# Rotary embedding of 16 heads: two of the early loads are issued in two halves each

## The chip, the core and the metric

The kernel runs on one core of a Trainium2 chip. Its time is device microseconds (us) of one launch; the time before is the median of three runs, 161.38 us (161.21 to 161.65). The core has five engines that matter here: TensorE (PE in the profile; PEld are its weight loads), VectorE (DVE), ScalarE (ACT), GpSimd (POOL) and SyncE (SP). Each runs its own list of instructions in order; semaphores tie the lists together. DMAs are issued by SyncE and by ScalarE, each through a queue of its own; both queues are served by the same 16 DMA engines.

## The reference

The input x has 16 batches of 512 positions and 1024 numbers, which are 16 heads of 64. Each head is split into two halves of 32, and the pair is rotated by tables that depend on the position:

```python
x = x.reshape(batch, seq, num_heads, head_dim)
x1, x2 = (x[..., :half_dim].copy(), x[..., half_dim:].copy())
cos = cos[None, :, None, :].copy()
sin = sin[None, :, None, :].copy()
rotated = np.concatenate([x1 * cos - x2 * sin, x1 * sin + x2 * cos], axis=-1)
```

All is fp32. 33.6 MB are read and 33.6 MB written, so for each number there are only two products and one sum.

## The kernel before

**Tiles.** A "row" (index u, 0 to 63) is one position's 1024 numbers on each of the 128 partitions, 4 KB per partition. A tile is a group of rows loaded and stored together. Batches 0, 1, 14 and 15 are single tiles of four rows per partition (16 KB, 2 MB in all): partition p holds positions 4p to 4p+3. The other twelve batches are loaded two at a time, six pair tiles of eight rows per partition (32 KB, 4 MB in all): partition 2s+b holds positions 8s to 8s+7 of the pair's batch b. That gives ten tiles: 0 and 1 are single, 2 to 7 are pairs, 8 and 9 single. In the SBUF there is a ring of 40 rows, `x_sb`, in which a tile is loaded, computed in place and stored from. Tiles 0 to 5 fill it; tiles 6 to 9 take the places of tiles 0 to 4 when those have been stored.

**Work on one row.** The result is t1 + t2, where t1 = x times cosine (L310) is written by VectorE into PSUM (`t1_ps`, three buffers), and t2 = x with its halves swapped, times minus or plus sine, is written into `t2_sb` (eight buffers). GpSimd makes t2 (L271), mostly two rows per instruction; for row 3 of every pair tile VectorE makes it (L303). The sum goes one of two ways: VectorE adds and writes back to the ring (`comb`, L321), or, for rows 1, 3 and 5 of each group of eight, TensorE adds t2 to the PSUM buffer by a matmul with the identity (L233) and ScalarE copies the sum to the ring (L200). VectorE does the product of row u before the sum of row u-1.

**Tables.** The tables come by two small DMAs into `stage`. For single tiles they are used as they come (ScalarE makes the signed sine, L191 and L192; VectorE copies the cosine, L281). For pair tiles the positions lie otherwise on the partitions, so TensorE moves the tables by matmuls with a selector (L217), which ScalarE has built from an identity (L186), and ScalarE makes the signed sine from that (L195, L196). Before the first row of tile 2 VectorE copies one row of the sine for its own products (L288, L289).

**Order of the DMAs.** SyncE issues the loads of tile 1, the sine table and tile 2 (`on_sync`, L161 to L163). After that it issues only stores: for each tile it waits for the last row's sum and issues one store of the whole tile (L169). ScalarE issues tile 0, the cosine table and tiles 3, 4 and 5 (`on_scalar`, L174 to L183) before its first computation; the loads of tiles 6 to 9 come later in its list, each after a wait for the stores that free the place (L203).

**Waits for a load.** Every tile has one semaphore, `sem_in[t]`, that its load raises by 16. GpSimd (L265) and VectorE (L296) wait for it before the first row of the tile. The other rows follow without a wait for the load.

Of the kernel before, what the change touches and what calls it, by code (L numbers as in the profile page):

```python
# [6 lines left out]
def bass_split_heads_rope_kernel(  # L7
# [21 lines left out]
    R1 = seq // P  # L29
# [11 lines left out]
    tiles = [(b, R1 if b in singles else R2) for b in range(batch) if b in singles or b % 2 == 0]  # L41
    NT = len(tiles)
    RING = 5 * R2
# [24 lines left out]
    EH = H * HD // BANK  # L68
    LEAD = 1
    LAG = 14  # L70

    with ExitStack() as stack:
        x_sb = stack.enter_context(nc.sbuf_tensor([P, RING, H, 2, HALF], fp32))
# [8 lines left out]
        pair_ps = stack.enter_context(nc.psum_tensor([P, 2, 2, R1, HALF], fp32))  # L82
        t1_ps = stack.enter_context(nc.psum_tensor([P, NT1, H * HD], fp32))
        sem_in = [stack.enter_context(nc.semaphore(f"in{t}")) for t in range(NT)]
        sem_out = [stack.enter_context(nc.semaphore(f"out{k}")) for k in range(EARLY)]
        sem_rest = stack.enter_context(nc.semaphore("rest"))
        sem_cos = stack.enter_context(nc.semaphore("cos"))
# [20 lines left out]
        x1 = x.rearrange("b (s r) d -> b s (r d)", r=R1)  # L108
        o1 = out.rearrange("b (s r) h d -> b s (r h d)", r=R1)
        x2 = x.rearrange("b (s r) d -> s b (r d)", r=R2)  # L110
# [3 lines left out]
        def in_dram(single, pairs, t):  # L114
            b, n = tiles[t]
            return single[b] if n == R1 else pairs[:, b:b + 2, :]

        def in_sbuf(t):
            b, n = tiles[t]
            k = b * R1 % RING  # L120
            return x_sb[:, k:k + n].rearrange("p n h t d -> p (n h t d)")

        def where(u):
            t, r = rows[u]
            return t, r, u % RING
# [25 lines left out]
            return sum(b * R1 // R2 == k for b, _ in tiles)  # L151

        def load(eng, t):
            eng.dma_start(in_sbuf(t), in_dram(x1, x2, t)).then_inc(sem_in[t], 16)  # L154

        def load_table(eng, i):
            table, sem = ((cos, sem_cos), (sin, sem_sin))[i]
            eng.dma_start(stage[:, i, :], table.rearrange("(s r) d -> s (r d)", r=R1)).then_inc(sem, 16)  # L158

        def on_sync(sp):  # L160
            load(sp, 1)  # L161
            load_table(sp, 1)
            load(sp, 2)  # L163
            for u in range(NU):
                t, r, k = where(u)
                if r == tiles[t][1] - 1:
                    wait_added(sp, u)
                    k = u // R2
                    sp.dma_start(in_dram(o1, o2, t), in_sbuf(t)).then_inc(sem_out[k] if k < EARLY else sem_rest, 16)  # L169
            sp.wait_ge(sem_rest, 16 * sum(stores_of(k) for k in range(EARLY, NU // R2)))  # L170

        def on_scalar(ae):
            later = {}
            for t, (b, n) in enumerate(tiles):  # L174
                if t in (1, 2):
                    continue
                if b * R1 + n <= RING:
                    load(ae, t)
                else:

                    later.setdefault((b * R1 - RING) // R2 * R2 + R2 - 1 + LAG, []).append(t)
                if t == 0:
                    load_table(ae, 0)  # L183

            ae.wait_ge(sem_i, 2)
            ae.activation(  # L186
                pick[:], ident[:].rearrange("q (s k) -> q k s", k=2)[:, :, :, None].broadcast_to([P, 2, P // 2, 2]), COPY
            ).then_inc(sem_g, 1)
            ae.wait_ge(sem_sin, 16)
            sv = stage[:, 1, :].rearrange("s (r d) -> s r d", d=HALF)  # L190
            ae.activation(s1_sb[:, :, 0, :], sv, COPY, scale=-1.0)  # L191
            ae.activation(s1_sb[:, :, 1, :], sv, COPY).then_inc(sem_s, 1)  # L192
            ae.wait_ge(sem_t, 2)
            s2 = s2_sb[:].rearrange("p (k r) t d -> p k r t d", r=R1)
            ae.activation(s2[:, :, :, 0, :], pair_ps[:, :, 1, :, :], COPY, scale=-1.0)  # L195
            ae.activation(s2[:, :, :, 1, :], pair_ps[:, :, 1, :, :], COPY).then_inc(sem_s, 1)  # L196
            for u in range(NU):
                if PE2[u]:
                    ae.wait_ge(sem_e, n_pe[u])
                    ae.activation(xs[:, u % RING, :], t1_ps[:, u % NT1, :], COPY).then_inc(sem_a, 1)  # L200
                for t in later.get(u, ()):
                    k = (tiles[t][0] * R1 - RING) // R2
                    ae.wait_ge(sem_out[k], 16 * stores_of(k))  # L203
                    load(ae, t)
# [38 lines left out]
        def on_gpsimd(pl):  # L243
            pl.memset(ident[:], 1.0).then_inc(sem_i, 1)  # L244
            pl.wait_ge(sem_i, 1)
            pl.affine_select(  # L246
                out=ident[:],
                in_=ident[:],
                compare_op=mybir.AluOpType.is_equal,
                fill=0.0,  # L250
                base=0,
                pattern=[[-1, P]],
                channel_multiplier=1,
            ).then_inc(sem_i, 1)
            for u in range(NU):
                if V2[u] or (G2[u] and u % 2 == 1):
                    continue
                t, r, k = where(u)
                n = 2 if G2[u] else 1
                if (t, r) == (0, 0):  # L260
                    pl.wait_ge(sem_s, 1)
                if (t, r) == (2, 0):
                    pl.wait_ge(sem_s, 2)
                if r == 0:
                    pl.wait_ge(sem_in[t], 16)  # L265
                if n == 2 and u + 1 >= NT2:
                    pl.wait_ge(sem_m, u + 2 - NT2 + NT1)
                elif n == 1:
                    wait_t2_free(pl, u)
                table = (s1_sb if tiles[t][1] == R1 else s2_sb)[:, r:r + n]  # L270
                pl.tensor_tensor(  # L271
                    t2_sb[:, u % NT2:u % NT2 + n],
                    x_sb[:, k:k + n, :, ::-1, :],
                    table[:, :, None, :, :].broadcast_to([P, n, H, 2, HALF]),
                    mult,
                ).then_inc(sem_p, 1)

        def on_vector(ve):
            ve.memset(zero[:], 0.0).then_inc(sem_z, 1)  # L279
            ve.wait_ge(sem_cos, 16)  # L280
            ve.tensor_copy(c1_ps, stage[:, 0, :].rearrange("s (r d) -> s r d", d=HALF)).then_inc(sem_c, 1)  # L281
            ve.wait_ge(sem_c, 1)
            ve.wait_ge(sem_w, NT1 * EH)

            def pair_tables():
                ve.wait_ge(sem_s, 2)
                row = pair_ps[:, V_ROW // R1, 1, V_ROW % R1, :]
                ve.tensor_scalar_mul(v_ps[:, 0, :], row, -1.0).then_inc(sem_c, 1)  # L288
                ve.tensor_copy(v_ps[:, 1, :], row).then_inc(sem_c, 1)  # L289

            first_v = V2.index(True)

            def mul(u):
                t, r, k = where(u)
                if r == 0:
                    ve.wait_ge(sem_in[t], 16)  # L296
                if (t, r) == (2, 0):
                    pair_tables()
                if u == first_v:
                    ve.wait_ge(sem_c, 3)  # L300
                if V2[u]:
                    wait_t2_free(ve, u)
                    ve.tensor_tensor(t2_sb[:, u % NT2, :, :, :], swapped(k), over_heads(v_ps), mult)  # L303
                if u >= NT1:
                    v = u - NT1
                    if PE2[v]:
                        ve.wait_ge(sem_a, n_pe[v])  # L307
                    else:
                        ve.wait_ge(sem_v, n_comb[v])
                ve.tensor_tensor(  # L310
                    t1_ps[:, u % NT1, :].rearrange("p (h d) -> p h d", d=HALF),
                    x_sb[:, k, :, :, :].rearrange("p h t d -> p (h t) d"),
                    c_of(t, r)[:, None, :].broadcast_to([P, 2 * H, HALF]),
                    mult,
                ).then_inc(sem_m, 1)

            def comb(u):
                t, r, k = where(u)
                ve.wait_ge(sem_m, u + 1)
                ve.wait_ge(sem_p, n_pool[u])  # L320
                ve.tensor_tensor(  # L321
                    xs[:, k, :],
                    t1_ps[:, u % NT1, :],
                    t2_sb[:, u % NT2, :, :, :].rearrange("p h t d -> p (h t d)"),
                    add,
                ).then_inc(sem_v, 1)

            for u in range(NU + LEAD):
                if u < NU:
                    mul(u)  # L330
                if u >= LEAD and not PE2[u - LEAD]:
                    comb(u - LEAD)
# [39 lines left out]
```

## Time and profile before

| what | value |
|---|---|
| median of three runs | 161.38 us (161.21 to 161.65) |
| the profiled execution | 161.49 us, of which the span from first to last instruction is 160.06 (160.1 on the page) |
| POOL, busy | 131.5 us (82% of the span) |
| DVE, busy | 129.6 us (81%) |
| PE, busy | 66.3 us (41%) |
| ACT, busy | 24.4 us (15%) |
| moved by DMA | 67.25 MB, mean 420 GB/s over the span |
| load of tile 2, issue to landing | 31.6 us |
| SyncE's wait for the last store, at the end | 10.8 us |

The page cuts the span into 40 slices of 4 us; a digit is the busy share of a slice in tenths, 9 being 90% or more. The DMA row is the mean of the 16 DMA engines. Under the queues stand packets, MB, and the time of their packets as a share of 16 engines' span; q1 is SyncE's queue and q10 ScalarE's. In the list in order of time a line has the start, the length, the engine, the line of the kernel and the operation, with the tile it writes, an arrow, and what it reads; the bracket gives the idle time before it and what ended it.

### The profile page before, as it was taken

What the parts mean: (1) busy time and instruction counts of PE and PEld (TensorE: products, weight loads), DVE (VectorE), ACT (ScalarE), POOL (GpSimd) and SP (SyncE); (2) the same over time, 40 slices, a digit from 0 to 9 for tenths busy, and PEclk for the clock granted to TensorE, in tenths of its full rate; (3) what the DMA queues carried; (4) which work ended last, traced back from release to release, by engine and by line L of the source; (5) the groups of instructions that cost most, each with busy time, mean ns of one, the idle gap of its engine ahead of it and who ended that gap; (6) DMA issues with size and microseconds to landing.
All of it is one profiled execution on the core that took longest, in us unless ns stands there. A gap on an engine that the chain in (4) does not pass through costs nothing.

```text
span 160.1 us, 499 instructions
## 1 busy us (share of the span) xinstructions
PE 66.3 (41%) x94; PEld 22.8 (14%) x94; DVE 129.6 (81%) x117; ACT 24.4 (15%) x27; POOL 131.5 (82%) x41
## 2 busy tenths in 40 slices
PE   6005000804760486058904892376148903920000
PEld 1002000202210221022302230222022302300000
DVE  0005994888999999999899989999999999899100
ACT  0401100110222022202220222022202220220000
POOL 1004999979999999999999999999999999994000
PEclk9999999975899579955696558579955696595555
DMA  5999999999999999999999999999999999999896
GB/s 184 426 434 430 450 459 401 393 393 414 438 475 442 393 418 436 475 434 393 434 483 393 401 508 401 401 442 414 455 450 438 438 414 454 409 409 475 373 446 278
DMA packets 3169, 67.25 MB, mean 420 GB/s; under 512 B 352, under 2 KB 608, under 8 KB 608
## 3 DMA queue, kind: packets, MB, share of 16 engines
q1 hardware_dynamic: 1872, 39.91, 58.4%
q10 hardware_dynamic: 1296, 27.33, 40.1%
q14 instruction: 1, 0.01, 0.0%
HBM read 33.69 MB, written 33.55 MB: 420 GB/s over the span
## 4 chain that ended last, share of the span: by engine, by line
DVE 46%; DMA 19%; PE 11%; issue 11%; POOL 3%; ACT 3%; SPq 1%; DVEq 0%
DVE t_ps L310 26%; DMA x_sb<-in_x_dram 19%; DVE x_sb L321 16%; PE t_ps L233 11%; DVE t_sb L303 5%; POOL t_sb L271 3%; ACT x_sb L200 3%; SPq L158 0%; SPq L154 0%; DVEq L320 0%; DVEq L307 0%
## 5 line engine op out<-in xcount | busy, mean ns | idle before, releaser
L271 POOL TENSOR_TENSOR t_sb<-x_sb,s_sb 128x2048 f32<-128x2048 f32 (+1 forms) x35 | 130.8, 3784 | 13.9 <-ACT s_sb L192 12.8
L233 PE MATMUL t_ps<-t_sb,ident 128*128 128x512 f32 x84 | 61.5, 883 | 63.8 <-DVE t_ps L310 44.9
L310 DVE TENSOR_TENSOR t_ps<-x_sb,pair_ps 128x1024 f32<-128x1024 f32 x48 | 57.5, 1221 | 1.2 <-ACT x_sb L200 1.2
L321 DVE TENSOR_TENSOR x_sb<-t_ps,t_sb 128x1024 f32<-128x1024 f32 x43 | 52.2, 1216 | 4.0 <-POOL t_sb L271 4.0
L200 ACT ACTIVATE x_sb<-t_ps 128x1024 f32<-128x1024 f32 x21 | 21.5, 1023 | 104.1 <-PE t_ps L233 104.1
L233 PEld LDWEIGHTS t_ps<-t_sb,ident 128*128 128x128 f32 x84 | 20.8, 274 | 104.3 <-DVE t_ps L310 74.0
L310 DVE TENSOR_TENSOR t_ps<-x_sb,tab_ps 128x1024 f32<-128x1024 f32 x16 | 19.2, 1221 | 0.5 <-ACT x_sb L200 0.5
L281 DVE COPY tab_ps<-stage 128x128 f32<-128x128 f32 x1 | 0.3, 294 | 12.5 <-DMA stage<-in_cos_dram 12.5
L303 DVE TENSOR_TENSOR t_sb<-x_sb,tab_ps 128x1024 f32<-128x1024 f32 x6 | 7.3, 1210 | 0.0
L217 PE MATMUL pair_ps<-stage,pick 128*128 128x256 f32 x4 | 2.0, 667 | 9.8 <-DMA stage<-in_cos_dram 9.8
L210 PE MATMUL t_ps<-zero 128*128 128x512 bf16 x6 | 2.7, 630 | 1.2 <-DVE zero L279 1.2
L217 PEld LDWEIGHTS pair_ps<-stage,pick 128*128 128x128 f32 x4 | 1.2, 326 | 10.9 <-issue 10.7
L186 ACT ACT_TABLE_LOAD x1 | 1.3, 1283 | 4.0 <-issue 4.0
L191 ACT ACTIVATE s_sb<-stage 128x128 f32<-128x128 f32 x1 | 0.3, 309 | 7.9 <-DMA stage<-in_sin_dram 7.9
L210 PEld LDWEIGHTS t_ps<-zero 128*128 128x128 bf16 x6 | 0.7, 137 | 2.3 <-DVE zero L279 1.2
L279 DVE MEMSET zero<- 128x256 uint32 x1 | 0.3, 272 | 0.9 <-PEq L354 0.9
L195 ACT ACTIVATE s_sb<-pair_ps 128x256 f32<-128x256 f32 x1 | 0.4, 383 | 1.8 <-PE pair_ps L217 1.8
L244 POOL MEMSET ident<- 128x128 f32 x1 | 0.2, 204 | 0.3 <-POOLq L354 0.3
L186 ACT ACTIVATE pick<-ident 128x256 f32<-128x256 f32 x1 | 0.4, 416 | 0.0
L196 ACT ACTIVATE s_sb<-pair_ps 128x256 f32<-128x256 f32 x1 | 0.4, 378 | 0.0
L246 POOL TENSOR_SCALAR_AFFINE_SELECT ident<-ident 128x128 f32<-128x128 f32 x1 | 0.3, 292 | 0.1
L354 POOL MEMSET const-float32-0.0<- 128x1 f32 x1 | 0.1, 99 | 0.3 <-issue 0.3
(6 smaller groups left out, 1.0 us busy)
## 6 DMA issues: line engine op xcount, KB each, us to landing
out_dram<-x_sb SPq DMA_DIRECT2D x6, 4096.0 KB, 26.0
x_sb<-in_x_dram ACTq DMA_DIRECT2D x5, 4096.0 KB, 31.8
out_dram<-x_sb SPq DMA_DIRECT2D x4, 2048.0 KB, 18.1
x_sb<-in_x_dram ACTq DMA_DIRECT2D x3, 2048.0 KB, 24.7
x_sb<-in_x_dram SPq DMA_DIRECT2D x1, 4096.0 KB, 31.6
x_sb<-in_x_dram SPq DMA_DIRECT2D x1, 2048.0 KB, 12.3
stage<-in_cos_dram ACTq DMA_DIRECT2D x1, 64.0 KB, 12.5
stage<-in_sin_dram SPq DMA_DIRECT2D x1, 64.0 KB, 12.3
```

The costliest lines, as they stand in the source:

```text
L186: ae.activation(pick[:], ident[:].rearrange("q (s k) -> q k s", k=2)[:, :, :, None].broadcast_to([P, 2, P // 2, 2]), COPY).then_inc(sem_g, 1)
L191: ae.activation(s1_sb[:, :, 0, :], sv, COPY, scale=-1.0)
L195: ae.activation(s2[:, :, :, 0, :], pair_ps[:, :, 1, :, :], COPY, scale=-1.0)
L196: ae.activation(s2[:, :, :, 1, :], pair_ps[:, :, 1, :, :], COPY).then_inc(sem_s, 1)
L200: ae.activation(xs[:, u % RING, :], t1_ps[:, u % NT1, :], COPY).then_inc(sem_a, 1)
L210: pe.matmul(t1_ps[:, k, b * BANK:(b + 1) * BANK], zero[:, 0:P], zero[:], start=True, stop=True).then_inc(sem_w, 1)
L217: pe.matmul(pair_ps[:, k].rearrange("p c r d -> p (c r d)"), pick[:, k].rearrange("q s b -> q (s b)"), stage[:].rearrange("q c f -> q (c f)"),
L233: ins = pe.matmul(t1_ps[:, u % NT1, b * BANK:(b + 1) * BANK], ident[:], t2[:, b * BANK:(b + 1) * BANK], start=False, stop=True, skip_group ...
L271: pl.tensor_tensor(t2_sb[:, u % NT2:u % NT2 + n], x_sb[:, k:k + n, :, ::-1, :], table[:, :, None, :, :].broadcast_to([P, n, H, 2, HALF]), ...
L303: ve.tensor_tensor(t2_sb[:, u % NT2, :, :, :], swapped(k), over_heads(v_ps), mult)
L310: ve.tensor_tensor(t1_ps[:, u % NT1, :].rearrange("p (h d) -> p h d", d=HALF), x_sb[:, k, :, :, :].rearrange("p h t d -> p (h t) d"), c_of ...
L321: ve.tensor_tensor(xs[:, k, :], t1_ps[:, u % NT1, :], t2_sb[:, u % NT2, :, :, :].rearrange("p h t d -> p (h t d)"), add,).then_inc(sem_v, 1)
```

## The change

The loads of tiles 2 and 3, the first and the second pair, are issued as two DMAs each. The first brings rows 0 to 3 of every partition (16 KB) and raises `sem_in[t]`; the second brings rows 4 to 7 (16 KB) and raises a new semaphore, `sem_low[t]`. The two halves of tile 2 follow each other on SyncE's queue, those of tile 3 on ScalarE's. GpSimd and VectorE wait for the first before row 0 and for the second before row 4. All other loads and all stores remain as they are; the order of the tiles on the two queues is the same.

```diff
+    ON_SYNC = (1, 2)
+    HALVED = (2, 3)
...
+        sem_low = {t: stack.enter_context(nc.semaphore(f"low{t}")) for t in HALVED}
...
         def load(eng, t):
-            eng.dma_start(in_sbuf(t), in_dram(x1, x2, t)).then_inc(sem_in[t], 16)
+            if t not in HALVED:
+                eng.dma_start(in_sbuf(t), in_dram(x1, x2, t)).then_inc(sem_in[t], 16)
+                return
+            w = x.shape[2]
+            k = tiles[t][0] * R1 % RING
+            for lo, sem in ((0, sem_in[t]), (R1, sem_low[t])):
+                rows_of = x_sb[:, k + lo:k + lo + R1].rearrange("p n h t d -> p (n h t d)")
+                eng.dma_start(rows_of, in_dram(x1, x2, t)[:, :, lo * w:(lo + R1) * w]).then_inc(sem, 16)
+
+        def wait_loaded(eng, t, r):
+
+            if r == 0:
+                eng.wait_ge(sem_in[t], 16)
+            elif r == R1 and t in HALVED:
+                eng.wait_ge(sem_low[t], 16)
...
         def on_sync(sp):
-            load(sp, 1)
-            load_table(sp, 1)
-            load(sp, 2)
+            for t in ON_SYNC:
+                load(sp, t)
+                if t == ON_SYNC[0]:
+                    load_table(sp, 1)
...
-                if t in (1, 2):
+                if t in ON_SYNC:
...
-                if r == 0:
-                    pl.wait_ge(sem_in[t], 16)
+                wait_loaded(pl, t, r)
...
-                if r == 0:
-                    ve.wait_ge(sem_in[t], 16)
+                wait_loaded(ve, t, r)
```

## The prediction

> **What bounds the kernel now.** I read four views, in this order: the page's slices of the span, its DMA queues, the busy time by stretches of the span, and the waits.
>
> The slices and the queues of the page come first:
>
> ```profile
> span 160.1 us, 499 instructions
> DVE  0005994888999999999899989999999999899100
> POOL 1004999979999999999999999999999999994000
> DMA  5999999999999999999999999999999999999896
> ...
> q1 hardware_dynamic: 1872, 39.91, 58.4%
> q10 hardware_dynamic: 1296, 27.33, 40.1%
> ...
> out_dram<-x_sb SPq DMA_DIRECT2D x4, 2048.0 KB, 18.1
> ```
>
> Three resources look full: VectorE (DVE), GpSimd (POOL) and the 16 DMA engines. Two of them begin late (POOL's digits are high from the fourth slice, some 14 us) and end early; the DMA row is 9 from the second slice to the 38th. The queues settle it. q1 carries SyncE's loads and all stores, q10 ScalarE's loads; their packets took 58.4% + 40.1% = 98.5% of 16 engines' span, 157.7 of 160.1 us. What is left is 2.4 us, the start before the first packet and the end after the last.
>
> A mean can hide a gap, so the stretches come next (columns: window, its length, the busy time of PE, PEld, DVE, ACT and POOL, the granted clock, DMA share, GB/s; the shares scatter around 1):
>
> ```profile
> 14.00:28.00 14.00, 1.84 (x4) 0.94 (x4) 11.67 (x12) 0.72 (x3) 13.85 (x6) 1.00 0.99 426
> 28.00:33.00 5.00, 3.40 (x4) 1.18 (x4) 4.01 (x4) 1.02 (x1) 4.37 (x1) 1.00 1.02 380
> 33.00:62.80 29.80, 14.06 (x22) 4.87 (x23) 29.04 (x28) 5.12 (x5) 29.36 (x8) 0.77 1.00 429
> 62.80:67.80 5.00, 1.14 (x3) 0.19 (x1) 5.00 (x6) 1.02 (x1) 5.00 (x2) 1.00 1.00 433
> ...
> 142.00:149.00 7.00, 0.00 (x0) 0.00 (x0) 6.79 (x7) 0.16 (x1) 4.02 (x2) 0.61 0.94 405
> 149.00:158.00 9.00, 0.00 (x0) 0.00 (x0) 0.00 (x0) 0.00 (x0) 0.00 (x0) 0.50 1.00 430
> ```
>
> From 149 to 158 us no compute engine works, and the DMA engines are as full as ever: a backlog of stores is being written. In the records of single packets 16 packets are in flight at every moment between 2.5 and 158.7 us. The stretch from 28 to 33 us is also full, but moves only 380 GB/s: there the last packet of each engine in the second load on SyncE's queue (tile 2) and in the one on ScalarE's (tile 3) took about 1.5 us, where 1.213 us is the usual time of a 32 KB packet.
>
> Last the chain that ended last and the instructions in order of time with their waits. In the chain the long piece at the start is the load of tile 2:
>
> ```profile
> 1.69 30.68 DMA x_sb<-in_x_dram
> ```
>
> In order of time (start, length, engine, line, and in brackets the idle time before it) these lines stand around it and at the end:
>
> ```profile
> 33.44 27.08 POOL L271 TENSOR_TENSOR t_sb<-x_sb,s_sb 128x2048 f32<-128x2048 f32 x7 [1.07 <-issue]
> 38.05 1.22 DVE L321 TENSOR_TENSOR x_sb<-t_ps,t_sb 128x1024 f32<-128x1024 f32 x1 [0.76 <-POOL t_sb L271]
> ...
> 148.86 0.34 SPq L169 DMA_DIRECT2D out_dram<-x_sb  x1
> ```
>
> POOL finishes tile 1 at 32.37, is idle 1.07 us and begins tile 2 at 33.44, when its load has landed (issued at 1.69, 31.6 us to landing by the page). It is POOL's only wait after 14.15. DVE in turn stood 0.76 us for POOL's result. But the last store, issued at 148.86, is over only at 160.0, 11.2 us later. What would it need alone? The first load of 2 MB took 12.3 us from issue to landing and shared the engines with another: 4.19 MB at the 412 GB/s of 2.5 to 12 us are 10.2 us, so 2.1 us are fixed. The last store alone needs 2.1 + 2.10 MB / 430 GB/s (4.9 us) = 7.0 us. So it stood some 4.2 us behind the store before it. Compute could end up to 4.2 us later at no cost, and ending earlier buys nothing.
>
> **The change part by part.**
>
> *Bytes and packets.* Tiles 2 and 3 are 8.39 MB together, today in 256 packets of 32 KB, then in 512 of 16 KB. The bytes stay. For the price of the smaller packet: 149 to 158 us holds almost only 16 KB packets and runs at 430 GB/s, 62.8 to 67.8 us 32 KB packets alone at 433 GB/s. 8.39 MB take 19.51 us at the one and 19.37 at the other, +0.14 us. The single packets say the same: 0.611 us against 1.213, so two halves cost 0.009 us more; 256 x 0.009 / 16 engines = 0.14 us. Nothing covers this, since the DMA engines are never free. Low end: the 380 GB/s of 28 to 33 us come back to 430, 5 x (1 - 380/430) = 0.58 us won. High end: the same loss at the end of each first half too, 0.58 us more. I take +0.14, nearest to what all other stretches do.
>
> *Two more DMAs.* Each adds one switch from one transfer to the next on its queue, and 16 semaphore packets of 0.009 us (one per engine). Between 149 and 158 us the queue goes from the store of tile 8 to that of tile 9 with nothing on the other queue, and 430 GB/s against 433 leaves at most 9 x 3/433 = 0.06 us for the switch, packet size included. I take 0.02 us for both DMAs; the ends are 0 and 2 x 0.06 = 0.12. [...]
>
> *Issuing.* SyncE issues one load more (0.39 us for a 16 KB one, 0.64 for a 32 KB one); its next act is a store at 24.78, so this is covered by more than 20 us. ScalarE's three pair loads took 2.21 us, 0.74 each; now there are four, at most 0.74 us more. Behind them stand the table load (now at 3.95), the building of the selector (ending at 5.67), and then 7.89 us of waiting for the sine table; even uncovered it would be 0.74 us on the start of POOL, which the 4.2 us at the end take up. The sine and cosine loads are issued before the halves and keep their place. No step passes another queue's work.
>
> *First half early.* Queues share evenly here: at 12.8 us tiles 2 and 3 begin, and the first two halves are 4.19 MB, at 426 GB/s 9.8 us. They land near 23 to 25 us; POOL asks at 32.37 and goes straight on. Its 1.07 us go, and with it DVE's 0.76. Next late is DVE itself: it adds row 6 from 32.47 and copies two table rows from 33.61, after POOL has restarted. So compute ends 0.76 to 1.07 us sooner, the last store is issued near 148.0 instead of 148.86, and waits that much longer behind the one before. On the path: 0.
>
> *Added waits.* POOL (four-row mark of tiles 2 and 3) and DVE wait on the second half. It lands where the whole did, near 33.5. POOL asks for tile 2's row 4 near 32.4 + 4.5 + 2.3 = 39.2, DVE later: covered by 5.7 us; tile 3's by over 10. If it were late, POOL's two-row products queue behind, and DVE's adds and TensorE's matmuls wait for them. A met wait costs about 0.017 us (SyncE's last semaphore instruction): four are 0.07, hidden too.
>
> *Sum*, against the profiled execution, 161.49 us (span 160.06 and 1.43 around it, 0.11 above the median of three): 160.06 + 0.14 + 0.02 = 160.22 of span, 161.65 in all; put on the median, 161.38 + 0.16 = 161.5.
>
> **The rivals.**
>
> *The chain is right, compute sets the end* (faster). The chain begins at tile 2's load, and the gain would be 0.76 to 1.07 us: 160.3 to 160.6. Against it: nine microseconds of stores after the last compute instruction, and the backlog of 4.2 us. Chance 0.07.
>
> *The slow stretch goes* (faster). If 28 to 33 us is slow because two 32 KB loads end together, the halves could mend it: 161.38 + 0.16 - 0.58 = 161.0, at the edge of 0.3%. For it: it lies just where the change works. Against it: loads that end at 47 and 62 us show no such loss, so the cause may lie outside the kernel. Chance 0.10.
>
> *Every end of a pair of loads is slow* (slower). If the same rows show that two loads ending side by side are served badly, there are now two such places: 161.38 + 0.16 + 0.58 = 162.1. It decides from 0.32 us of added loss on, since 0.48 us is 0.3%. For it: both slow packet groups are the last of their loads. Against it: the loads of tiles 0 and 1 also end side by side, near 12 us, without it. Chance 0.20.
>
> *Both queues stand still at the switch* (slower). The halves end at nearly the same time on both queues, so a start-up as long as at the beginning (2.1 us) would find nothing to fill it: 163.6. Against it: at 12 to 14 us both queues change transfers twice and the engines stay full. Chance 0.05, with the form in which every added DMA pays its 2.1 us alone (4.2 us, 165.7) among it. [...]
>
> *The halves change nothing*, because the first lands no sooner than the whole, gives 161.5 as well, and is within the forecast.
>
> **How the numbers follow.** The forecast (DMA stays the bound, +0.16 us) has the rest, 0.58, with a range of its own of 161.2 to 161.8; runs of one kernel here spread over 0.44 us, and 0.3%, 0.48 us, is about what a measurement can tell from no change. Faster: 0.07 and half of the 0.10, 0.12. Slower: 0.20 + 0.05 = 0.25. Same: 0.58 and the other half, 0.63. The range from 160.7 to 162.4 leaves out the first rival and the last and holds the two in between.
>
> **What would show it.** Right: the DMA row stays 9 throughout, packet time stays near 157.9 us, POOL's idle of 1.07 us before 33.44 is gone, the last store is issued near 148.0 and takes near 12 us to land. Wrong: a DMA slice below 9 around 22 us (a stall at the switch), a rate well under 420 GB/s between 14 and 33 us (half rows read badly), or an end that moves forward with the last store's issue (compute was the bound).

## The result: 163.49 us, and the profile after

The changed kernel takes 163.49 us (median of six, 162.60 to 163.74) against 161.41 us before (six runs, 161.16 to 162.16): a ratio of 1.011, 95% interval 1.0075 to 1.0145 (the measurement's own estimate, here and below, and not the quotient of the medians). That is slower, by some 2 us, and outside the forecast range of 160.7 to 162.4.

The page of the changed kernel, the lines that answer to those of before:

```profile
span 160.3 us, 505 instructions
DVE  0005994899989999999999989998999999899100
POOL 1004999999999999999999999999999998795000
DMA  5999999999999999999999999999999999999895
...
q1 hardware_dynamic: 2016, 39.91, 58.3%
q10 hardware_dynamic: 1440, 27.33, 40.1%
...
out_dram<-x_sb SPq DMA_DIRECT2D x4, 2048.0 KB, 18.7
```

The span has hardly moved: 160.28 us where it was 160.06. The queues carry 288 packets more (256 of data, 32 of semaphores) in the same share of time. But the execution that this profile shows took 163.37 us, 3.09 more than its span; before it was 161.49 and 1.43. In all six executions of the changed kernel the time around the span is 2.61 to 3.14 us. So most of the loss does not lie where the change works: some 1.5 us of it lie outside the span, where the page has no line at all. The rest, some 0.5 us, is within the scatter of the spans: the six were 159.8 to 161.0 with a median of 160.4, and in the second measurement below the median is 160.05, against 159.9 to 160.0 before.

The stretches of the changed kernel (columns as before):

```profile
14.00:28.00 14.00, 1.82 (x5) 0.95 (x5) 11.69 (x12) 0.70 (x3) 13.88 (x6) 1.00 1.01 431
28.00:33.00 5.00, 3.75 (x4) 1.13 (x4) 4.01 (x4) 1.02 (x1) 5.00 (x2) 1.00 1.04 416
33.00:62.80 29.80, 16.73 (x23) 5.92 (x24) 29.39 (x29) 5.12 (x5) 29.80 (x8) 0.89 1.00 427
...
149.00:158.00 9.00, 0.00 (x0) 0.00 (x0) 0.00 (x0) 0.00 (x0) 0.00 (x0) 0.50 0.99 426
```

Full as before (share 0.99 to 1.04 in these four, where it was 0.99 to 1.02), with no hole near 22 us where the halves change over, and the stretch from 28 to 33 us is a little better than before (416 against 380 GB/s). The list in order of time, around the places that the forecast named:

```profile
14.12 121.69 POOL L288 TENSOR_TENSOR t_sb<-x_sb,s_sb 128x1024 f32<-128x1024 f32 x32 [12.75 <-ACT s_sb L210]
137.29 9.14 POOL L288 TENSOR_TENSOR t_sb<-x_sb,s_sb 128x2048 f32<-128x2048 f32 x3 [1.48 <-DMA x_sb<-in_x_dram]
...
148.87 0.34 SPq L187 DMA_DIRECT2D out_dram<-x_sb  x1
```

POOL now runs from 14.12 to 135.81 without a pause: the 1.07 us ahead of tile 2 are gone. It then waits 1.48 us for the load of tile 9, the last one, whose data packets end at 135.67 and whose last semaphore packet at 136.88, no sooner than before (135.23 and 136.44). The last store is issued at 148.87, before at 148.86.

The trace also records DMA packets outside the span. Some bear the kind "instruction" (q14 on the page), which is read here as a fetch of instructions. Larger than 40 bytes and after the start there are these (not a view of the profile; listed from the records):

```
kernel    queue  start us  took us  bytes
before    q14      60.28     0.31    8192
changed   q14      63.00     0.31    8192
changed   q8      162.18     1.50   16384
```

In the changed kernel a packet of 16 KB is fetched 1.90 us after the span has ended, on a queue that carries nothing else, and takes 1.50 us. It is over 3.40 us behind the span, where 3.09 us lie around the span; at which moments the launch's time starts and stops the trace does not show, so the two need not agree.

### The profile page after: what moved, and what is told of

Its sections match the earlier page's. It is cut to its first block, busy times and chain, and to the rows that moved or that the text cites. A ratio compares the mean times of both kernels' runs of the same rounds, so it can differ in the third digit from the quotient of the medians.

```text
span 160.3 us, 505 instructions
## 1 busy us (share of the span) xinstructions
PE 68.3 (43%) x94; PEld 23.4 (15%) x94; DVE 129.7 (81%) x117; ACT 24.4 (15%) x27; POOL 131.5 (82%) x41
## 4 chain that ended last, share of the span: by engine, by line
DMA 33%; DVE 24%; POOL 12%; issue 11%; PE 10%; ACT 3%; SPq 0%; DVEq 0%; ACTq 0%
DMA x_sb<-in_x_dram 25%; DVE t_ps L326 12%; POOL t_sb L288 12%; PE t_ps L251 10%; DVE x_sb L337 9%; DMA stage<-in_sin_dram 8%; DVE t_sb L319 3%; ACT x_sb L218 3%; SPq L158 0%; ACT s_sb L209 0%; ACT s_sb L210 0%; DVE tab_ps L305 0%; DVEq L336 0%; DVE tab_ps L306 0%; ACTq L158 0%
## 5 line engine op out<-in xcount | busy, mean ns | idle before, releaser
L251 PE MATMUL t_ps<-t_sb,ident 128*128 128x512 f32 x84 | 63.5, 911 | 60.9 <-DVE t_ps L326 48.7
L251 PEld LDWEIGHTS t_ps<-t_sb,ident 128*128 128x128 f32 x84 | 21.5, 282 | 102.8 <-DVE t_ps L326 72.0
```

The costliest lines, as they stand in the source:

```text
L251: ins = pe.matmul(t1_ps[:, u % NT1, b * BANK:(b + 1) * BANK], ident[:], t2[:, b * BANK:(b + 1) * BANK], start=False, stop=True, skip_group ...
```

## The experiments

Three theories. **List**: the added instructions lengthen some engine's list so that a last block of instructions is fetched after the span, and the core waits for it. **Transfers**: two more DMAs cost something outside the span. **Semaphores**: two more semaphores cost something there. The change does all three: counted in the compiled program, GpSimd's list goes from 58 to 60 instructions, VectorE's from 175 to 177, ScalarE's from 40 to 41, SyncE's from 27 to 28; TensorE's stays at 208. The traces record one or two fewer on each engine (57 and 59 on GpSimd) and show the same differences.

All results in one table; "around" is time minus span, as the median of the executions. The kernel before, run beside each, had medians of 161.35 to 161.46 and 1.43 around (1.38 to 1.48). Each row has ten executions, the first measurement six, "four waits" four and "two waits, GpSimd" eight.

| kernel | GpSimd's list | us | ratio to before, 95% | span | around |
|---|---|---|---|---|---|
| changed, first measurement | 60 | 163.49 | 1.011 (1.0075 to 1.0145) | 160.4 | 2.95 |
| changed, again | 60 | 162.69 | 1.0055 (1.0031 to 1.0079) | 160.05 | 2.68 |
| halves, one semaphore | 58 | 161.32 | 1.0012 (0.9989 to 1.0034) | 159.9 | 1.42 |
| two idle semaphores | 58 | 161.44 | 1.0014 (0.9998 to 1.0031) | 160.0 | 1.43 |
| four waits | 60 | 162.53 | 1.0076 (1.0059 to 1.0093) | 159.95 | 2.55 |
| two waits, VectorE | 58 | 161.34 | 0.9997 (0.9982 to 1.0012) | 159.9 | 1.41 |
| two waits, GpSimd | 60 | 162.76 | 1.0081 (1.0058 to 1.0104) | 159.95 | 2.86 |
| one wait, GpSimd | 59 | 161.33 | 0.9995 (0.9975 to 1.0015) | 159.9 | 1.42 |
| changed, rows joined | 58 | 161.36 | 0.9992 (0.9970 to 1.0015) | 159.9 | 1.45 |
| before, rows joined | 56 | 161.36 | 0.9995 (0.9983 to 1.0007) | 159.95 | 1.42 |
| many waits, GpSimd | 78 | 161.39 | 0.9998 (0.9986 to 1.0009) | 159.95 | 1.44 |
| changed, many waits | 78 | 161.55 | 1.0011 (0.9994 to 1.0028) | 160.15 | 1.41 |
| six waits, GpSimd | 64 | 161.52 | 1.0009 (0.9995 to 1.0022) | 160.0 | 1.46 |
| ten waits, GpSimd | 68 | 161.36 | 0.9991 (0.9978 to 1.0005) | 159.9 | 1.44 |
| many waits, ScalarE | 58 | 161.50 | 1.0020 (1.0004 to 1.0037) | 160.1 | 1.41 |
| GpSimd starts late | 58 | 161.52 | 1.0016 (0.9999 to 1.0033) | 160.1 | 1.41 |

Three kernels, in four measurements, have a list of 60, and they alone are slow by the median. One other stands out around the span: of the ten executions of the kernel with a list of 64, three have 1.81, 1.88 and 1.93 us there, the other seven 1.37 to 1.48.

### The change taken apart

The transfers alone: both halves raise the tile's one semaphore, and both engines wait for all of it before row 0.

```diff
+            for lo in (0, R1):
...
+                eng.dma_start(rows_of, in_dram(x1, x2, t)[:, :, lo * w:(lo + R1) * w]).then_inc(sem_in[t], 16)
...
-                    pl.wait_ge(sem_in[t], 16)
+                    pl.wait_ge(sem_in[t], 32 if t in (2, 3) else 16)
...
-                    ve.wait_ge(sem_in[t], 16)
+                    ve.wait_ge(sem_in[t], 32 if t in (2, 3) else 16)
```

> Tiles 2 and 3 are loaded in two halves each, but both halves raise the tile's one semaphore and GpSimd and VectorE wait for all 32 before row 0: the transfers of the change without its two semaphores and without its four added waits. Instructions against the kernel before: ScalarE and SyncE one more each, GpSimd, VectorE and TensorE as many. Theory of the longer list (an engine's list is now long enough that a last block of instructions is fetched after the span): back at 161.4 us if GpSimd's or VectorE's list is the one, about 163.4 if ScalarE's or SyncE's; about 1.4 us or 3.0 us around the span. Theory of the transfers (more DMAs and packets cost at the end): 163.4. Theory of the semaphores (each semaphore costs at the end): 161.4. Span in all cases 160.0 to 160.6.

Measured 161.32 us. The four loads of half the size are worth nothing that can be told from zero. The theory of the transfers falls, and with it the lists of ScalarE and SyncE, which are one longer here.

The semaphores alone, taken ahead of the others and never used:

```diff
+        spare = [stack.enter_context(nc.semaphore(f"low{t}")) for t in (2, 3)]
```

> The kernel before with two more semaphores taken and never used, so that those behind them get the same numbers as in the changed kernel; no instruction more on any engine. Theory of the semaphores: 163.4 us, 3.0 around the span. Theory of the longer list and theory of the transfers: 161.4, 1.4 around the span. Span 160.1.

Measured 161.44 us, 1.43 around: the theory of the semaphores falls.

The waits alone, on whole loads:

```diff
                 if r == 0:
                     pl.wait_ge(sem_in[t], 16)
+                elif r == R1 and t in (2, 3):
+                    pl.wait_ge(sem_in[t], 16)
...
                 if r == 0:
                     ve.wait_ge(sem_in[t], 16)
+                elif r == R1 and t in (2, 3):
+                    ve.wait_ge(sem_in[t], 16)
```

> The kernel before with whole loads, and on GpSimd and on VectorE one wait more before row 4 of tiles 2 and 3, for the semaphore of the whole load, which is long met: two instructions more on each of the two engines, nothing else. Theory of the longer list: 163.4 us if GpSimd's or VectorE's list is the one, with a packet of 16 KB after the span; else 161.4. Theories of the transfers and of the semaphores: 161.4. Span 160.1 in all cases.

Measured 162.53 us with a span of 159.95. The packet records of its profile again hold 16 KB on q8, at 161.84 us, 0.93 us long. Four waits that never wait cost 1.2 us, nearly all of it around the span (2.55 against 1.43), which has not grown.

Of these only the two on VectorE:

```diff
                 if r == 0:
                     ve.wait_ge(sem_in[t], 16)
+                elif r == R1 and t in (2, 3):
+                    ve.wait_ge(sem_in[t], 16)
```

> As the kernel with the four waits, but the two on VectorE alone. Theory of the longer list: 163.4 us if it is VectorE's list, 161.4 if it is GpSimd's, ScalarE's or SyncE's. The others: 161.4. Span 160.1.

Measured 161.34 us. And only the two on GpSimd:

```diff
                 if r == 0:
                     pl.wait_ge(sem_in[t], 16)
+                elif r == R1 and t in (2, 3):
+                    pl.wait_ge(sem_in[t], 16)
```

> The kernel before with the two added waits on GpSimd alone (its list two instructions longer, all others as long as before). Theory of GpSimd's list (the two instructions more make it fetch a last block of 16 KB after the span): 162.5 us as with all four waits, a packet of 16 KB about 1.9 us after the span's end, 2.5 us around the span. Rival (it takes the waits of both engines together, by what they do to the order of the work): 161.4 and 1.4 around the span. Span 160.0.

Measured 162.76 us, with the packet on q8 at 161.81 us (1.21 us long). It is GpSimd's list. One wait instead of two:

```diff
+                elif (t, r) == (2, R1):
+                    pl.wait_ge(sem_in[t], 16)
```

> The kernel before with one added wait on GpSimd, before row 4 of tile 2: its list is one instruction longer. Theory of GpSimd's list: all or nothing, 162.5 us if the 59th instruction is over the edge, 161.4 if it is the 60th. Rival (each wait has a price of its own): 161.95, half of what two cost. Span 160.0.

Measured 161.33 us, no packet behind the span. The median changes all at once, between 59 and 60 instructions.

### The change kept, the list shortened

Tile 0's four rows are made in two GpSimd instructions of two rows; the list is 58 long again, the halves and their waits stay.

```diff
-        return u % 2 == 0 and R1 <= u < NU - 2 and not V2[u + 1]
+        return u % 2 == 0 and u < NU - 2 and not V2[u + 1]
```

> The changed kernel with all of its halves, semaphores and waits, but with GpSimd making the four rows of tile 0 in two instructions of two rows instead of four of one, so that its list is as long as before the change. Theory of GpSimd's list: 161.5 us (the 161.4 of before and the 0.1 to 0.2 of the smaller packets), no packet after the span, 1.4 around the span. Rival (halves and waits cost something together): 163.4, 3.0 around the span. Span 160.2.

Measured 161.36 us against 161.37 before: the loss is gone and no gain stands in its place. The last store is issued sooner in this profile than before (148.86), by as much as the forecast said:

```profile
147.88 0.34 SPq L187 DMA_DIRECT2D out_dram<-x_sb  x1
```

The span of that execution is 160.49 us, no shorter for it. The control, the same edit to the kernel before:

> The kernel before with the rows of tile 0 joined in twos on GpSimd, as in the changed kernel with the shorter list; GpSimd's list is two instructions shorter than before the change, nothing else differs. It is the control for the joined version: if joining wins time by itself, the 161.36 us of that version could hide a loss by the halves. Theory of GpSimd's list: 161.4, as before, 1.4 us around the span. Rival (a shorter list or the joining gains by itself): 160.8 or less.

Measured 161.36 us. Joining gains nothing by itself, so the halves neither lose nor win beside it. The changed kernel itself on the same chip:

> The changed kernel itself on the chip of the others, for the 1.0 us between it (163.5) and the kernel with the four waits alone (162.5). Theory of GpSimd's list alone: the fetch costs the same in both, and the 1.0 us lies in the chip or in where the list happens to be placed: 162.5 to 162.7 here. Rival (the halves add a cost of their own once the list is over the edge): 163.5 here. Span 160.2.

Measured 162.69 us. Here the change costs 1.3 us, not 2.1; the series ran on several chips, and whether the chip makes this difference was not tried. In three of the ten executions only 1.7 us lay around the span, in the other seven 2.6 to 2.9. In its profile the packet came at 163.02 us, again 1.90 after the span's end, and took 1.20 us.

### Longer lists

If one more block costs, a list of 78 should cost as much as one of 60.

```diff
+                elif r != R1 - 1:
+                    pl.wait_ge(sem_in[t], 16)
```

> The kernel before with a wait, long met, on GpSimd before nearly every instruction on rows: its list is 20 instructions longer. Theory of GpSimd's list (one more block is fetched, whatever the number of instructions in it): 162.6 to 162.9 us as with two waits. Rival (the waits themselves cost, 0.7 us each as the two did): over 170. Span 160.0, at most 160.4.

Measured 161.39 us: neither theory had that. Twenty instructions more cost nothing, where two cost 1.2 to 1.4 us. The queues of its page show one fetch of instructions more inside the span (queue: packets, MB, share; the first fence is the four-waits kernel, the second this one):

```profile
q14 instruction: 1, 0.01, 0.0%
```

```profile
q14 instruction: 2, 0.02, 0.0%
```

A second fetch of 8 KB now lies within the span, by the packet records at 125.93 us; the kernel before has only the first, at 60.28. So the theory was put again as one of place: the block is fetched at some place of the list, and the core waits for it only where that place falls behind the last instruction of the kernel. If that is right, the changed kernel gets faster by being made longer:

```diff
                 wait_loaded(pl, t, r)
+                if r != 0 and r != R1 - 1:
+                    pl.wait_ge(sem_in[t], 16)
```

> The changed kernel, halves, semaphores and waits, with 18 more long-met waits on GpSimd, so that its list has 78 instructions where the changed kernel has 60. Theory of the place (the block is fetched at a fixed place of the list, and only where that falls behind the span's end does the core stand for it): 161.4 to 161.6 us, faster than the changed kernel by more than 1 us though it does more; no packet of 16 KB after the span, instead one more 8 KB packet of instructions within the span, near 126 us as in the kernel of 78 before; 1.4 us around the span. Rival (the halves and their waits keep a cost of their own): 162.7 or more. Span 160.0 to 160.5.

Measured 161.55 us, the second fetch at 123.42 us. Here POOL never waits after its first instruction, and the last store leaves 0.96 us sooner than before, without a gain in the time:

```profile
147.90 0.34 SPq L187 DMA_DIRECT2D out_dram<-x_sb  x1
```

Between 60 and 78:

```diff
+                elif (r != R1 - 1 and u < 24):
+                    pl.wait_ge(sem_in[t], 16)
```

> The kernel before with six long-met waits on GpSimd, a list of 64. Theory of the place: no sum but one of two values, 161.4 us with the fetch inside the span or 162.6 to 162.8 with the packet of 16 KB behind it; four instructions beyond 60, the place is still behind the span's end if the engine's closing instructions run there one by one, so 162.7 is likelier. Rival (it depends on the number of waits): between the two. Span 160.0.

```diff
+                elif (r != R1 - 1 and u < 36):
+                    pl.wait_ge(sem_in[t], 16)
```

> As the kernel with a list of 64, with ten waits, a list of 68. Theory of the place: 161.4 or 162.7 us, and 161.4 if the one of 64 is already there; with both at 162.7 the cost goes between 68 and 78. Rival: between the two. Span 160.0.

Measured 161.52 us with 64 and 161.36 with 68. The likelier value expected for 64 was wrong; the closing instructions of the engine, on which it rested, were not shown: the traces of the kernel before and of the changed kernel record none on GpSimd behind its last product. With 68 the fetch is recorded at 150.64 us, within the span and behind POOL's last work; with 64 the profiled execution has no second fetch inside the span and none behind it, but it is one of the seven that lost nothing; of the three with 1.81 to 1.93 us around the span there is no trace. From 68 to 78 instructions the fetch moves earlier as the list grows. Between 60 and 64 most of the cost goes, and at 68 all of it. The lists of 60 were measured on two chips of the series (the chip of the first measurement is not on record), those of 64, 68 and 78 on two others, on which no list of 60 was run; that these would have shown the loss too is assumed.

ScalarE's list made longer than 60 (the 48 added waits became 24 instructions in the compiled list):

```diff
-            ae.wait_ge(sem_sin, 16)
+            for _ in range(49):
+                ae.wait_ge(sem_sin, 16)
```

> The kernel before with many waits, all for the sine table, on ScalarE where there was one: its list is 24 instructions longer, 64 against 40, and so longer than the 60 of GpSimd that cost time. Is the edge GpSimd's alone? If every engine has the same closing instructions behind its list: 162.5 us or more, with a packet of 16 KB after the span. If the edge is another on ScalarE: 161.4 and no such packet. Span 160.1, the waits being met at 13.5 us within some 0.5 us, which compute can spare.

Measured 161.50 us with 64 instructions on ScalarE, 1.41 around and no packet behind the span; one more 8 KB packet at 147.59 us. No cost around the span at that length there; the small excess of the ratio, 1.0020 (1.0004 to 1.0037), lies in the span (median 160.1 us against 160.0). Where ScalarE's edge lies, if it has one, is not known.

### Does compute set the end?

The forecast rests on the claim that compute has some 4 us to spare. GpSimd's first wait is raised from one event to two, so that it starts when the tables of the pair tiles are made:

```diff
                 if (t, r) == (0, 0):
-                    pl.wait_ge(sem_s, 1)
+                    pl.wait_ge(sem_s, 2)
```

> The kernel before in which GpSimd's first product waits for the sine table of the pair tiles too, so that GpSimd starts some 2.4 us later (near 16.5 instead of 14.15 us); no instruction more or less. It tries the forecast's step that compute has some 4 us to spare at the end. Theory (the DMA engines set the end of the span): 161.4 to 161.6, span 160.1. Rival (compute sets it): 163.8, span 162.5.

In order of time, the kernel before begins with this line:

```profile
14.15 18.22 POOL L271 TENSOR_TENSOR t_sb<-x_sb,s_sb 128x1024 f32<-128x1024 f32 x6 [12.79 <-ACT s_sb L192]
```

The list in order of time and the stretch at the end, of this kernel:

```profile
16.72 121.66 POOL L271 TENSOR_TENSOR t_sb<-x_sb,s_sb 128x1024 f32<-128x1024 f32 x32 [15.36 <-ACT s_sb L196]
138.89 9.14 POOL L271 TENSOR_TENSOR t_sb<-x_sb,s_sb 128x2048 f32<-128x2048 f32 x3 [0.51 <-DMA x_sb<-in_x_dram]
...
150.96 0.34 SPq L169 DMA_DIRECT2D out_dram<-x_sb  x1
```

```profile
149.00:158.00 9.00, 0.00 (x0) 0.00 (x0) 1.89 (x2) 0.00 (x0) 0.00 (x0) 0.50 0.99 422
```

POOL starts 2.57 us later, the last store is issued 2.10 us later, and the median is 161.52 against 161.38, a ratio of 1.0016 (0.9999 to 1.0033). Of the 2.10 us at most some 0.5 reach the end. The DMA engines, as full from 149 to 158 us as before (share 0.99 and 422 GB/s, before 1.00 and 430), set it.

## Why the prediction was wrong

**What bounds the span: right.** DMA share is near 1 in all stretches of the changed kernel from 2.5 to 158 us (0.95 to 1.05); of a delay of 2.6 us on GpSimd at most 0.5 us reach the end, and a last store that left 0.96 to 0.98 us sooner (the joined and the longest version of the changed kernel, 161.36 and 161.55 us) gained nothing. That compute has all of the 4.2 us to spare was not measured; the delay of the last store was 2.1.

**Bytes and packets, +0.14 us, and two more DMAs, +0.02: in line, but too small to be shown.** The span of the profiled execution went from 160.06 to 160.28, forecast 160.22; with spans of 159.8 to 161.0 in the six executions, so close a match is luck. The transfers alone gave 1.0012 (0.9989 to 1.0034), and the joined version 0.9992 (0.9970 to 1.0015): 0.1% is inside both, and so is nothing. The packets' time over 16 engines was 157.74 before and 157.73 after. In the profile of the changed kernel neither switch between halves shows a hole: on SyncE's queue the last packet of the first half ends at 22.20 us and the first of the second starts at 22.22, on ScalarE's at 22.81 and 22.84. That each added DMA pays 2.1 us of its own, as the form with 165.7 us has it, no run shows: the transfers alone measured 161.32 us.

**The slow stretch.** It did not double: from 14 to 28 us, where the first halves end, the rate is 431 GB/s, and their last packets took at most 0.62 us, little over the 0.61 that is the median of all 16 KB packets. It did not go away either. From 28 to 33 us the five profiles with halves show 383 to 416 GB/s (median 397), the twelve with whole loads 364 to 406 (median 380); the two overlap. The last packets of tile 3's second half took 0.76 to 0.90 us at the median, in place of 0.61, in all five. Neither rival was met; why packets are slow near 30 us stays open.

**First half early: half right.** POOL's 1.07 us and DVE's 0.76 went as said. The step "the last store is issued near 148.0" held in two of the four profiles with halves and their waits (147.88 and 147.90) and failed in the other two (148.87 and 149.48). What was late in these was the load of the last tile, for which POOL stood 1.48 and 2.21 us. That load's last data packet ends anywhere from 133.5 to 136.3 us in these four profiles, and from 134.5 to 136.2 in those with whole loads (the kernel in which GpSimd starts late left out): it scatters from profile to profile, with and without the change.

**Issuing: right.** The longer issue costs no wait that the span shows; the table load of ScalarE moved from 3.95 to 4.4 us, ahead of a wait of 7.4. One price was too low: SyncE's two halves took 0.65 and 0.87 us to issue, not the 0.39 of the single tile's load.

**Added waits: the step that failed.** It priced four met waits at 0.017 us each, "hidden too". In the span no more is seen: 159.95 us with the four waits alone, where it was 159.9 to 160.0. Their place in GpSimd's list was not priced, and it cost 1.2 us with the four waits alone, 1.4 with GpSimd's two, 1.3 in the changed kernel measured again and some 1.5 of the 2.1 in its first measurement. The sum failed with it at the term "1.43 around it", which was carried over as if it could not change: it became 2.6 to 3.1, and 1.7 to 2.9 when the changed kernel was measured again. No rival spoke of the time outside the span.

What is shown: two more instructions on GpSimd bring the loss, with whole loads and without the new semaphores (162.76 us); taking two others away removes it with the halves in place (161.36); with eighteen more, on another chip, it is not there (161.55); it lies around the span, and the four profiles that have it have a 16 KB packet behind the span:

| profile | starts after the span's end | packet took | around the span | around less packet |
|---|---|---|---|---|
| changed, first measurement | 1.90 | 1.50 | 3.09 | 1.59 |
| changed, again | 1.90 | 1.20 | 2.79 | 1.59 |
| four waits | 1.90 | 0.93 | 2.53 | 1.60 |
| two waits, GpSimd | 1.88 | 1.21 | 2.80 | 1.59 |

What is left without the packet is the same in all four, and 0.16 us more than the 1.43 of the kernel before. That the core waits for this packet is an inference from these times, if a strong one: packet and loss come together, and each tenth of a microsecond of the packet is found again in the loss. That the packet holds GpSimd's instructions is inferred too, from which list brings it. Beyond these packets the traces do not show in what pieces a list is fetched. The added fetches inside the span, 8 KB each at 123, 126 and 151 us, cost nothing that can be measured (ratios 1.0011, 0.9998 and 0.9991), while the one of 16 KB behind it came with 1.10 to 1.66 us more around the span. Open stays why the fetch behind the span is one packet of 16 KB on a queue of its own while those within are 8 KB on q14, why three of ten executions with a list of 64 lost 0.4 to 0.5 us and the others nothing, and why three of ten of the changed kernel, measured again, lost only 0.3 us around the span.

## What to carry to other kernels

Set the time of a launch against the span before explaining a difference: when the span stands still, as here with the four waits (159.95 us, and 1.1 of the 1.2 us lay around it), look for the cause outside it. Count the instructions that a change adds to each engine's list, also those that cost nothing where they run: two on GpSimd cost 1.4 us here. The loss was absent here both with a shorter list (58) and with a longer one (78, on another chip), and there with 60, which points to a place in the list; joining instructions elsewhere on that engine mended it (162.69 to 161.36 us). And loading in smaller pieces to start an engine sooner gained nothing here, with the DMA engines full from 2.5 to 158 us: the engine either stood for a later load instead (1.48 and 2.21 us), or ended sooner and its last store stood longer behind the others (12.0 and 12.6 us from its issue to the end of the span, 11.2 before).

## What was not expected of the hardware

- A list of 60 instructions on GpSimd cost 1.2 to 1.4 us, with the waits alone, over one of 58 or 59. Lists of 68 and 78 cost nothing, and one of 64 cost 0.4 to 0.5 us in three of ten executions.
- A second fetch of instructions within the span, 8 KB like the first (which took 0.31 us), cost nothing that can be measured with lists of 68 and 78 on GpSimd (161.36 to 161.55 us); 16 KB behind it took 0.93 to 1.50 us, and the time around the span less that packet was 1.59 to 1.60 us in all four profiles.
- The time around the span is 1.38 to 1.48 us in all 110 executions of the kernel before beside the series, so steady that a microsecond more in it is plain in one run.
